# A hybrid decoder layer on eight cores: weight loads from a rearranged layout, early projections in one-bank pieces, and a last output tile in parts

## The chip, the cores and the metric

The kernel runs on all 8 cores of one Trainium2 chip. Every core has the same program and its own data: one prompt sequence of 2048 tokens and 16 sample tokens. The metric is the device time of the slowest core in microseconds (us).

A program on all cores has a second, slower state in some executions: the cores of one die get a lower clock, and the run is longer by a tenth or more. A median is over all runs of its kernel, so it can hold a slow one; the text says where. Tile numbers count from 0, so "tile 15" is the sixteenth and last full tile. TensorE is the matrix engine, VectorE, ScalarE and GpSimd the other compute engines, and SyncE (SP) here only issues transfers and waits for them. SBUF is the on-chip memory that holds the operands; PSUM is the memory that TensorE writes its results to, in banks that hold 512 fp32 columns here. In the profile their names are PE (PEld for weight loads), DVE, ACT, POOL and SP; a "q" after a name means the engine's sequencer (the part that issues transfers, waits and runs control instructions).

## The reference, cut to what matters

```python
def hybrid_layer(x, mem_k, mem_v, ...):              # x: (tokens, 1024) fp32
    u = rmsnorm(x, norm_g)
    proj = u @ w_in                                  # 8704 columns = 68 blocks of 128
    lx, lg, sb, scg, sh, sg, q, qg, mg = jnp.split(proj, SPLIT_POINTS, axis=-1)
    # A: causal conv(4) over lx, gated linear recurrence, times silu(lg), @ lru_wo
    # B: sb * causal conv(3) over (scg*sh), times silu(sg), @ sconv_wo
    # C: 4-head attention of q into 256 memory tokens, times silu(qg), @ xa_wo
    # [cut] the three branches are merged by sigmoid gates made from mg,
    # then one output projection @ w_out, the residual, and a final rmsnorm
```

Outputs are the normalised tokens (`y_prompt`, `y_sample`), the memory keys and values, and the new recurrence and convolution states. All are fp32; the matmuls run in bf16.

## The kernel before

The kernel records all its operations as tasks with a planned duration and a priority. Its own list scheduler then fixes one order per engine when the program is built. Where the next instruction of such a list has to wait, what stands behind it is held up with it; the run without pieces below shows what that costs TensorE (15.4 us of waits for scaled input tiles in the first 70 us, against 9.7 with pieces).

The input tiles. Each of the 16 prompt tiles (128 tokens) and the sample tile is loaded, squared and summed on ScalarE, given its reciprocal root on GpSimd (`rstd`), scaled, and transposed by eight TensorE instructions into `uT`.

```python
        def rstd(col, nr, prio):
            st = stat[0:nr, col:col + 1]
            G.pool(lambda e: e.tensor_scalar(out=st, in0=st, scalar1=1.0 / D, scalar2=EPS, op0=ALU.mult, op1=ALU.add),
                   0.2, [t_st[col]], [t_st[col]], prio)
            t_rs.append(G.pool(lambda e: e.tensor_tensor(out=st, in0=st, in1=cst[0:nr, 2:3], op=ALU.pow), 0.5,
                               [t_st[col], m_cst.t], [t_st[col]], prio))

        def p0(ti, src, nr, dst, gcols, tdst, prio, wait):
            x_, xn_, ps = Handle(xring), Handle(xnring), Handle(PS)      # PS: ring of 4 buffers of two PSUM banks
            # [cut] load from SP's queue, Square with sum on ScalarE, rstd on GpSimd,
            # scale on VectorE or GpSimd, 8 transposes, evacuation with gain on VectorE
```

The weights. GpSimd issues the load of a block of 128 columns of `w_in`, with a cast from fp32 to bf16. For each of 128 partitions and 8 row groups, it has 128 values in a row: 1024 pieces of 256 bytes as written.

```python
        def wload(ap, prio):
            k = ap.shape[1]
            hw = Handle(w2ring if 2 <= state["nw"] < 6 else wring)
            G.dma("pool", [(lambda: hw.ap[:, 0:k * 128].rearrange("p (k c) -> p k c", k=k), ap)], k * 65536 * 1.18, [], [hw.tok], prio, None)
            # [cut]

        def w_in_cols(c0):
            return w_in.rearrange("(k p) c -> p k c", p=128)[:, :, c0:c0 + 128]

        def unit(lhs, nk, rhs, u, reads, prio, hold=(), split=False):
            ps = Handle(PS)
            # [cut] 688 token columns as two halves of 344 (one PSUM bank each), 8 matmuls per half;
            # three such units cover the 2064 tokens
```

The last stage takes the 16 prompt tiles in order and the sample tile last.

```python
        for ti in range(17):
            # [cut] 16 matmuls of 512 columns, residual on VectorE, Square with sum on ScalarE
            rstd(col, nr, P)
            last = G.dve(lambda e, y_=y_, nr=nr, col=col: e.scalar_tensor_tensor(
                out=y_.ap[0:nr, :], in0=y_.ap[0:nr, :], scalar=stat[0:nr, col:col + 1], in1=fgb[0:nr, :], op0=ALU.mult, op1=ALU.mult), 1024,
                [y_.tok, t_st[col], m_fgb.t], [y_.tok], P)
            G.dma("sp", [(dst, lambda y_=y_, nr=nr: y_.ap[0:nr, :])], nr * 4096, [y_.tok], [], P, None)

        G.run(S, verbose)
        S.finish(block)     # then the program ends: every engine drains and meets the others at a barrier
```

The softmax here doesn't subtract the row's maximum and nothing guards it: scores larger than these inputs give would overflow.

Of the kernel before, what the change touches and what calls it, by code (L numbers as in the profile page):

```python
# [32 lines left out]
KVP = 10  # L33

# [121 lines left out]
class Ring:  # L156
    def __init__(self, name, aps, toks, sem=None):
        self.name = name
        self.aps = aps
        self.toks = toks  # L160
        self.sem = sem
        self.n = len(aps)
        self.avail = [0.0] * self.n
        self.busy = [False] * self.n


class Handle:
    __slots__ = ("ring", "phys", "left", "tok", "last")

    def __init__(self, ring):  # L170
        self.ring = ring
        self.phys = None
        self.left = 0
        self.last = 0.0
        self.tok = Tok(ring.name, handle=self)

    @property
    def ap(self):
        return self.ring.aps[self.phys]
# [13 lines left out]
class Graph:  # L193
# [85 lines left out]
    def dma(self, q, pairs, nbytes, reads, writes, prio, sem):  # L279
        return self._add(q, (0.95 if q == "pool" else 0.45) * len(pairs), None, reads, writes, prio, dma=(pairs, nbytes, sem))  # L280
# [29 lines left out]
    def run(self, S, verbose=False):  # L310
# [11 lines left out]
        while left:  # L322
            best = None
            for e, cands in ready.items():
# [5 lines left out]
                for t in cands:  # L330
# [3 lines left out]
                    for h in t.hs:  # L334
                        if h.phys is None:
                            a = 1e18
                            ring = h.ring
                            for i in range(ring.n):
                                if not ring.busy[i] and ring.avail[i] < a:
                                    a = ring.avail[i]  # L340
                            if a > r:
                                r = a
# [22 lines left out]
            for h in t.hs:  # L365
                if h.phys is None:
                    ring = h.ring
                    i = min((i for i in range(ring.n) if not ring.busy[i]), key=lambda i: ring.avail[i])
                    ring.busy[i] = True
                    h.phys = i  # L370
# [13 lines left out]
            if t.dma is not None:  # L384
                q, o = ("sw", "hw") if t.eng == "pool" else ("hw", "sw")
                a, n = max(dmafree[q], end + 0.8), t.dma[1] / 240e3
                both = min(2 * n, max(0.0, dmafree[o] - a))
                dmafree[q] = a + n + both / 2
                fin = dmafree[q] + 2.3
            for h in t.hs:  # L390
                h.left -= 1
                h.last = max(h.last, fin)
                if h.left == 0:
                    h.ring.busy[h.phys] = False
                    h.ring.avail[h.phys] = h.last
# [8 lines left out]
            mp = lambda k: k if k.handle is None else k.handle.ring.toks[k.handle.phys]  # L404
            reads, writes = [mp(k) for k in t.reads], [mp(k) for k in t.writes]
# [17 lines left out]
def build_program(verbose=False):  # L423
# [13 lines left out]
    st_h = din("st_h", [TS, W])  # L437
    st_lc = din("st_lc", [TS, 3 * W])
    st_sc = din("st_sc", [TS, 2 * W])
    norm_g = din("norm_g", [D])  # L440
    mem_norm_g = din("mem_norm_g", [D])
    w_in = din("w_in", [D, IN_COLS])
    lru_conv_w = din("lru_conv_w", [4, W])
    lru_conv_b = din("lru_conv_b", [W])
    lru_wa = din("lru_wa", [NCH, 128, 128])
    lru_ba = din("lru_ba", [W])
    lru_wx = din("lru_wx", [NCH, 128, 128])
    lru_bx = din("lru_bx", [W])
    lru_lambda = din("lru_lambda", [W])
    lru_wo = din("lru_wo", [W, D])  # L450
    sconv_w = din("sconv_w", [3, W])
    sconv_wo = din("sconv_wo", [W, D])
    xa_wk = din("xa_wk", [D, XW])
    xa_wv = din("xa_wv", [D, XW])
    xa_wo = din("xa_wo", [XW, D])
# [7 lines left out]
    o_ph = dout("o_ph", [1, W])  # L463
    o_plc = dout("o_plc", [3, W])
    o_psc = dout("o_psc", [2, W])
    o_sh = dout("o_sh", [TS, W])
    o_slc = dout("o_slc", [TS, 3 * W])
    o_ssc = dout("o_ssc", [TS, 2 * W])

    es = ExitStack()  # L470
    with es:
# [108 lines left out]
        def ring(name, mems, dma=False):  # L580
            if dma:
# [5 lines left out]
        PS = Ring("psum", [p[:] for p in psum], [Tok(f"psum{i}") for i in range(4)])  # L587
# [17 lines left out]
        m_prg = Mem("prg", PERM + 1792, 128, F32)  # L605
        m_prt = Mem("prt", PERM + 2304, 128, F32)
        prg, prt = m_prg.ap[0:16, :], m_prt.ap[0:66, :]
        t_pg = m_pT.tok("pTg")
        dsem("prg")
        dsem("prt")  # L610
        G.dma("sp", [(prg[0:8, :], norm_g.rearrange("(r c) -> r c", c=128)), (prg[8:16, :], mem_norm_g.rearrange("(r c) -> r c", c=128))],
              8192, [], [m_prg.t], -190, "prg")
        h = Handle(PS)
        G.pe([lambda e, h=h: e.transpose(h.ap[:, 0:16], prg, ident[0:16, 0:16])], 0.1, [m_prg.t, m_ident.t], [h.tok], -150)
        G.dve(lambda e, h=h: e.tensor_copy(pT[:, 0:16], h.ap[:, 0:16]), 16, [h.tok], [t_pg], -150)

        def params():
            plist = [(lru_conv_w, 0, 24, "k (n c) -> (k n) c"), (lru_conv_b, 24, 6, None), (lru_ba, 30, 6, None),
                     (lru_bx, 36, 6, None), (lru_lambda, 42, 6, None), (sconv_w, 48, 18, "k (n c) -> (k n) c")]
            G.dma("sp", [(prt[r0:r0 + nr, :], v.rearrange(pat, c=128) if pat else v.rearrange("(r c) -> r c", c=128))  # L620
                         for v, r0, nr, pat in plist], 42000, [], [m_prt.t], 20, "prt")
            G.after(G.tasks[-1], t_xd[10])
            h = Handle(PS)
            G.pe([lambda e: e.transpose(h.ap[:, 0:66], prt, ident[0:66, 0:66])], 0.3, [m_prt.t, m_ident.t], [h.tok], 30)
            G.dve(lambda e: e.tensor_copy(pT[:, 16:82], h.ap[:, 0:66]), 66, [h.tok], [m_pT.t], 30)


        def wload(ap, prio):
            k = ap.shape[1]
            hw = Handle(w2ring if 2 <= state["nw"] < 6 else wring)  # L630
            G.dma("pool", [(lambda: hw.ap[:, 0:k * 128].rearrange("p (k c) -> p k c", k=k), ap)], k * 65536 * 1.18, [], [hw.tok], prio, None)
# [5 lines left out]
        def w_in_cols(c0):  # L637
            return w_in.rearrange("(k p) c -> p k c", p=128)[:, :, c0:c0 + 128]

        def unit(lhs, nk, rhs, u, reads, prio, hold=(), split=False):  # L640
# [6 lines left out]
            if split:  # L647
                for b in range(2):
                    c = u * UW + b * BLK
                    t = G.pe([mm(k, b) for k in range(nk)], nk * 0.1465, [r for r in reads if r not in t_uT] + utoks(c, c + BLK), [ps.tok],  # L650
                             prio + 0.1 * b)
                    t.xgate = [t_tr[i] for i in range(17) if i * 128 < (u + 1) * UW] if b == 0 else []
            else:
                G.pe([mm(k, b) for k in range(nk) for b in range(2)], nk * 2 * 0.1465, reads, [ps.tok], prio, hold)
# [10 lines left out]

        def proj(c0, prio, lead=30.0, hold=((), (), ())):
            hw, lhs = pre.pop(c0) if c0 in pre else wload(w_in_cols(c0), prio - lead)
            return [unit(lhs, KC, uT, u, [hw.tok] + usl(u), prio + 2.4 * u, hold[u], prio < 60) for u in range(NU)]
# [27 lines left out]
        def p0(ti, src, nr, dst, gcols, tdst, prio, wait):  # L696
            x_, xn_, ps = Handle(xring), Handle(xnring), Handle(PS)
# [12 lines left out]
            def tr(kc):  # L710
# [6 lines left out]
                [ps.tok, t_pg], [tdst], prio)  # L717
# [5 lines left out]
        for i in range(17):  # L723
            if i >= 6:
                wait = [w_toks[min(i - 5, len(w_toks) - 1)]]
            elif i >= 3:
                wait = [x_toks[i - 3]]
            else:
                wait = []
            nr = 128 if i < 16 else TS  # L730
            src = xp[i * 128:(i + 1) * 128, :] if i < 16 else xs[:, :]
            x_toks.append(p0(i, src, nr, uT[:, :, i * 128:i * 128 + nr], pT[:, 0:8], t_uT[i], -100 + i, wait))
            while len(w_toks) < len(first) and len(w_toks) <= i:
                hw, lhs = wload(w_in_cols(first[len(w_toks)]), -100 + i)
                pre[first[len(w_toks)]] = hw, lhs
                if len(w_toks) >= 1:
                    G.after(G.tasks[-1], t_rs[i])
                w_toks.append(hw.tok)
                last = G.tasks[-1]
# [4 lines left out]
        params()  # L744


        m_sin = Mem("sin", m_xc.off, 4608, F32)
        sin = m_sin.ap
        for k in ("sin", "out"):
            dsem(k)  # L750
        t = G.dma("sp", [(sin[0:TS, 0:2304], st_lc[:, :]), (sin[0:TS, 2304:3072], st_h[:, :]),
                      (sin[0:TS, 3072:4608], st_sc[:, :])], 300000, [], [m_sin.t], 25, "sin")
        G.after(t, t_xd[15])
        o_slc3 = o_slc.rearrange("b (k c) -> b k c", k=3)
        st_lc3 = st_lc.rearrange("b (k c) -> b k c", k=3)
        o_ssc3 = o_ssc.rearrange("b (k c) -> b k c", k=2)
        st_sc3 = st_sc.rearrange("b (k c) -> b k c", k=2)
        t_dram = [Tok(f"dram{i}") for i in range(8)]
        t = G.dma("sp", [(o_slc3[:, 0:2, :], st_lc3[:, 1:3, :]), (o_ssc3[:, 0:1, :], st_sc3[:, 1:2, :])], 150000,
                  [], [t_dram[0]], 30, "out")  # L760
        G.after(t, t_rs[18])
        blocks_ = []
        for n in range(NCH):
            blocks_ += [k * W + n * 128 for k in range(3)] + [2304 + n * 128] + [3072 + k * W + n * 128 for k in range(2)]
        h = Handle(PS)
        t_sit = []
        for g0 in (0, 18):
            def trs(gi, g0=g0, h=h):
                c0 = blocks_[g0 + gi]
# [531 lines left out]
```

## Time and profile before

| | before |
|---|---|
| time, median of 3 runs | 767.55 us (767.3 to 767.73) |
| span of the profiled core (core 7, the slowest) | 764.4 us |
| TensorE busy | 719.3 us (94%) |
| sum of TensorE's work at its undisturbed pace | 700.4 us |
| time lost on TensorE by 60 / 110 / 400 us | 29.7 / 34.0 / 54 us |
| last matmul ends | 755.8 us |
| from there to the end | 8.6 us |

The fourth and fifth rows are worked out from the trace. A matmul in an undisturbed series starts a fixed time after the one before it (56 ns at 128 columns, 146 at 344, 216 at 512). The sum over all matmuls is the work. "Lost" is the time that has passed less the work done by then; half-clock time counts as lost too. This is a better ledger than "busy", because a matmul at half clock is busy twice as long.

These lines are from the page of the kernel before. They are the span, each engine's busy time with its instruction count, the shares of the chain of waits, the group of `w_in` loads as GpSimd issues them (busy us, mean ns of one | idle time before), and the same loads with size and us from issue to landing.

```profile
span 764.4 us, 12999 instructions; the slowest of 8 cores (758.2 to 764.4 us)
...
PE 719.3 (94%) x4771; PEld 456.5 (60%) x4771; DVE 403.8 (53%) x386; ACT 345.0 (45%) x408; POOL 246.4 (32%) x303
...
PE 85%; DMA 6%; ACT 4%; issue 2%; DVE 2%; POOL 1%; SPq 0%; POOLq 0%; ACTq 0%; DVEq 0%
...
L134 POOL DMA_DIRECT2D R<-w_in x68 | 61.5, 904 | 262.5 <-PE PP L645 250.7
...
R<-w_in POOLq DMA_DIRECT2D x68, 256.0 KB, 5.1
```

TensorE carries the kernel. The 6% of DMA in the chain lie in the head, and one issue of a weight load costs GpSimd 904 ns.

The queue table of the first 70 us of before: packets, MB, and the time that the packets took as a share of the 16 DMA engines.

```profile
q0 software_dynamic: 13819, 3.49, 56.2%
q1 hardware_dynamic: 2767, 9.55, 41.3%
```

The two shares add up to 97.5%, so transfers bind the head. The software queue (the weights, issued by GpSimd) moves 3.5 MB in 13,819 packets and takes more of the engines than the 9.6 MB of the hardware queue. The mean packet of 256 bytes took 46 ns there; over the whole run, the mean packet of 2048 bytes on the same queue took 201 ns, so eight times the bytes in 4.4 times the time. The Trainium skill, "DMA: Bandwidth & Descriptors", Specifications, says that transfers below 512 bytes miss the line rate; this trace agrees.

Three stretches of before, from the view of busy time by stretch: the stretch in us, its length, then busy us (and instructions) of PE, PEld, DVE, ACT and POOL, the granted TensorE clock, the DMA share and GB/s.

```profile
20.00:30.00 10.00, 7.08 (x36) 4.41 (x37) 4.13 (x4) 0.00 (x0) 4.22 (x6) 1.00 0.96 158
30.00:60.00 30.00, 26.53 (x205) 17.78 (x204) 13.71 (x12) 15.62 (x26) 17.32 (x27) 0.95 1.10 190
...
110.00:400.00 290.00, 276.89 (x1805) 175.64 (x1806) 184.79 (x151) 213.47 (x215) 46.28 (x63) 0.99 0.32 31
```

From 20 to 30 us TensorE did 36 matmuls and from 30 to 60 us 205, while the DMA engines were full.

Two lines of before's timeline of TensorE: start us, us taken, engine, line, operation, out<-in, count, and in brackets the idle time before it and what ended it.

```profile
24.74 5.52 PE L645 MATMUL PP<-R 128*128 128x344 bf16 x20
...
67.04 0.61 PE L711 MATMUL PP<-R 128*128 128x128 bf16 x8 [0.79 <-POOL R L703]
```

The first projection starts only at 24.74 us, and its 20 matmuls take 276 ns each, almost twice their undisturbed 146: the array is at half clock. The Trainium skill, "TensorE: Matmul & The Clock Gate", Part 1, says that the array runs at half rate until it has had some 3.4 us of sustained work. The trace agrees in kind: on the eight cores the first matmul at full pace came between 26.2 and 29.8 us, 2.0 to 5.0 us after the core's first projection had begun. The second line is the transposes of the last full input tile.

```profile
L141 SPq EVENT_SEMAPHORE  x54: 17/17/17, 761.5 to 764.1; - x54
...
L471 POOLq DRAIN  x1: 3108/3108/3108, 759.0 to 759.0; - x1
...
L471 SPq DRAIN  x1: 7/7/7, 764.2 to 764.2; - x1
```

A drain is the instruction that stands last in each engine's list, ahead of the closing barrier; in these traces none ends before its engine's last operation. SP's drain comes at 764.2 us, 8.4 us after the last matmul. The last store had landed 1.15 us before that, at 763.0: what lasted was SP's list of 54 waits, which SP took 2.69 us to step through (0.05 us each) once it had issued that store, though none of them held it up. All eight cores show the same. GpSimd's drain takes 3.1 us, or 2.55 us after its last operation (759.04 + 0.53). It is over at 762.1, two microseconds before SP gets to its own: it costs nothing here.

### The profile page before, as it was taken

The page shows a single profiled execution, that of the slowest core. Times are in us where ns is not written, and L with a number is a line of the kernel's source. Part 1 is how long each engine was busy: PE and PEld are TensorE (multiplying, and loading weights), DVE is VectorE, ACT ScalarE, POOL GpSimd, SP SyncE. Part 2 cuts the span into 40 slices and gives each one's busy share as a digit, 9 for nine tenths or more (in the row PEclk, how much of TensorE's full clock was granted, in tenths as well). Part 3 has the DMA queues.
Part 4 walks back from the last instruction along what each step waited for, and adds up shares of the span by engine and source line. Part 5 has one row for each costly group of instructions (what it writes and reads, how often), then busy time and mean ns, then how long its engine had stood idle before and what let it go on. Part 6 is the DMA issues. An engine that isn't in the chain of part 4 may idle for free.

```text
span 764.4 us, 12999 instructions; the slowest of 8 cores (758.2 to 764.4 us)
## 1 busy us (share of the span) xinstructions
PE 719.3 (94%) x4771; PEld 456.5 (60%) x4771; DVE 403.8 (53%) x386; ACT 345.0 (45%) x408; POOL 246.4 (32%) x303
## 2 busy tenths in 40 slices
PE   2889999989999989989999999999999999999995
PEld 1556656556566646646666666666666666665442
DVE  3354343846749638736976789842223122223765
ACT  4247379686696587687663211121111211112332
POOL 5555201201202102102114256553555464423221
PEclk9999999999999999999999999999999999999998
DMA  9999944412512332403324588865294849036933
GB/s 198 173 193 164 134 87 43 43 15 28 52 19 28 32 34 28 41 8 39 39 22 83 55 170 175 181 94 56 26 147 53 123 48 86 6 121 213 301 142 141
DMA packets 108601, 69.48 MB, mean 91 GB/s; under 512 B 94003, under 2 KB 96197, under 8 KB 108523
## 3 DMA queue, kind: packets, MB, share of 16 engines
q0 software_dynamic: 97760, 31.60, 39.7%
q1 hardware_dynamic: 10779, 37.06, 14.3%
q8 instruction: 39, 0.64, 0.3%
q14 instruction: 23, 0.19, 0.1%
HBM read 90.53 MB, written 9.82 MB: 131 GB/s over the span
## 4 chain that ended last, share of the span: by engine, by line
PE 85%; DMA 6%; ACT 4%; issue 2%; DVE 2%; POOL 1%; SPq 0%; POOLq 0%; ACTq 0%; DVEq 0%
PE PP L645 73%; PE PP L1227 8%; DMA R<-xp 3%; DMA R<-w_in 3%; PE PP L994 2%; ACT R L848 1%; PE PP L986 1%; DVE R L835 1%; ACT R L989 1%; ACT R L699 0%; POOL R L693 0%; POOL R L703 0%; PE PP L771 0%; PE PP L1122 0%; ACT R L832 0%
## 5 line engine op out<-in xcount | busy, mean ns | idle before, releaser
L645 PE MATMUL PP<-R 128*128 128x344 bf16 x4104 | 615.3, 311 | 6.8 <-ACT R L848 4.0
L645 PEld LDWEIGHTS PP<-R 128*128 128x128 bf16 x4104 | 401.7, 98 | 215.4 <-issue 16.2
L1179 ACT ACTIVATE R<-PP 128x688 f32<-128x688 f32 x72 | 53.6, 744 | 210.0 <-PE PP L645 205.2
L134 POOL DMA_DIRECT2D R<-w_in x68 | 61.5, 904 | 262.5 <-PE PP L645 250.7
L1188 DVE SCALAR_TENSOR_TENSOR R<-R,PP 128x688 f32<-128x688 f32 x72 | 62.3, 869 | 137.9 <-PE PP L645 130.0
L1227 PE MATMUL PP<-R 128*128 128x512 bf16 (+1 forms) x272 | 59.0, 379 | 0.0
L1192 POOL TENSOR_TENSOR R<-R 128x688 f32<-128x688 f32 x24 | 41.2, 1721 | 39.8 <-DVE R L1188 38.0
L1197 POOL TENSOR_TENSOR R<-R 128x688 bf16<-128x688 f32 x24 | 40.0, 1689 | 18.6 <-DVE R L1188 17.2
L1227 PEld LDWEIGHTS PP<-R 128*128 128x128 bf16 (+1 forms) x272 | 26.4, 97 | 32.2 <-issue 0.4
L835 DVE SCALAR_TENSOR_TENSOR R<-R 128x2048 f32<-128x2048 f32 x18 | 42.3, 2349 | 5.4 <-ACT R L832 4.2
L1236 ACT ACTIVATE R<-R 128x1024 f32<-128x1024 f32 (+1 forms) x17 | 18.0, 1057 | 46.3 <-DVE R L1231 46.3
L714 DVE TENSOR_TENSOR R<-PP,R 128x1024 bf16<-128x1024 bf16 (+1 forms) x19 | 22.2, 1174 | 21.4 <-PE PP L711 18.8
L711 PE MATMUL PP<-R 128*128 128x128 bf16 (+1 forms) x152 | 14.1, 248 | 19.2 <-DVE R L703 14.2
L1231 DVE SCALAR_TENSOR_TENSOR R<-PP,R 128x1024 f32<-128x1024 f32 (+1 forms) x17 | 20.8, 1224 | 20.6 <-PE PP L1227 20.6
L691 POOL TENSOR_SCALAR R<-R 128x1 f32<-128x1 f32 (+1 forms) x36 | 8.0, 222 | 72.8 <-ACT R L1236 44.5
L890 DVE TENSOR_TENSOR R<-PP,R 128x688 f32<-128x688 f32 x18 | 15.6, 873 | 28.1 <-PE PP L645 28.1
L848 ACT ACTIVATE R<-PP,R 128x688 f32<-128x688 f32 x36 | 27.4, 835 | 5.0 <-PE PP L645 5.0
L896 DVE SCALAR_TENSOR_TENSOR R<-R 128x2048 f32<-128x2048 f32 x12 | 28.2, 2346 | 0.9 <-ACT R L893 0.7
L862 DVE TENSOR_TENSOR_SCAN R<-R 128x2048 f32<-128x2048 f32 x6 | 26.5, 4421 | 0.4
L699 ACT ACTIVATE R<-R 128x1024 bf16<-128x1024 f32 (+1 forms) x19 | 20.1, 1056 | 14.6 <-DMA R<-xp 14.4
L1002 DVE TENSOR_TENSOR R<-PP,R 128x512 f32<-128x512 f32 x16 | 11.0, 687 | 27.0 <-ACT R L1000 27.0
L711 PEld LDWEIGHTS PP<-R 128*128 128x128 bf16 (+1 forms) x152 | 11.0, 111 | 23.3 <-issue 23.0
(133 smaller groups left out, 579.5 us busy)
## 6 DMA issues: line engine op xcount, KB each, us to landing
R<-w_in POOLq DMA_DIRECT2D x68, 256.0 KB, 5.1
R<-xp SPq DMA_DIRECT2D x32, 512.0 KB, 6.6
R<-ck SPq DMA_DIRECT2D x16, 512.0 KB, 4.7
y_p<-R SPq DMA_DIRECT2D x16, 512.0 KB, 3.0
R<-cv POOLq DMA_DIRECT2D x16, 256.0 KB, 7.5
R<-w_out POOLq DMA_DIRECT2D x8, 256.0 KB, 7.8
R<-xa_wo POOLq DMA_DIRECT2D x14, 128.0 KB, 4.1
R<-lru_wo POOLq DMA_DIRECT2D x8, 192.0 KB, 4.8
```

The costliest lines, as they stand in the source:

```text
L134: eng.dma_start(out=out, in_=in_).then_inc(sems[semkey], 16)
L645: return lambda e: e.matmul(ps.ap[:, b * 512:b * 512 + BLK], lhs(k), rhs[:, k, c:c + BLK], start=(k == 0), stop=(k == nk - 1))
L711: return lambda e: e.transpose(ps.ap.bitcast(BF16)[:, kc * 128:kc * 128 + nr], xn_.ap[0:nr, kc * 128:(kc + 1) * 128], identb[0:nr, 0:nr])
L835: G.dve(lambda e, k=k: e.scalar_tensor_tensor(out=xc[:, 0:T], in0=lxp[:, k:k + T], scalar=cw(k), in1=xc[:, 0:T], op0=ALU.mult, op1=ALU.add ...
L848: G.act(lambda e, ps=ps, dst=dst, u=u, bcol=bcol: e.activation(out=cols(dst, u), in_=pv(ps), func=AF.Tanh, scale=0.5, bias=dv[:, bcol:bcol ...
L862: G.dve(lambda e: e.tensor_tensor_scan(out=xc[:, 0:T], data0=thr[:, 0:T], data1=thi[:, 0:T], initial=0.0, op0=ALU.mult, op1=ALU.add), T, t ...
L896: G.dve(lambda e, k=k: e.scalar_tensor_tensor(out=cy[:, 0:T], in0=cinp[:, k:k + T], scalar=sw(k), in1=cy[:, 0:T], op0=ALU.mult, op1=ALU.ad ...
L1179: G.act(lambda e, ps=pg[u], th_=th_: e.activation(out=b3(th_.ap), in_=pv(ps), func=AF.Tanh, scale=0.5), UW, [pg[u].tok], [th_.tok], Px - E ...
L1188: G.dve(lambda e, zp=zp, th_=th_, dst=dst: e.scalar_tensor_tensor(out=b3(dst.ap), in0=b3(th_.ap), scalar=1.0, in1=pv(zp), op0=ALU.add, op1 ...
L1192: G.pool(lambda e, acc=acc, th_=th_: e.tensor_tensor(out=acc.ap, in0=acc.ap, in1=th_.ap, op=ALU.add), 1.6, [acc.tok, th_.tok], [acc.tok], Px)
L1197: G.pool(lambda e, acc=acc, th_=th_, u=u, j=j: e.tensor_tensor(out=mT[:, j, u * UW:(u + 1) * UW], in0=acc.ap, in1=th_.ap, op=ALU.add), 1.6 ...
L1227: return lambda e: e.matmul(ps.ap[0:nr, b * 512:(b + 1) * 512], mT[:, k, c0:c0 + nr], wo[:, k, b * 512:(b + 1) * 512], start=(k == 0), sto ...
```

## The change

The intent has four parts.

1. The host rearranges the weights, so that a `w_in` block is 128 rows of 2048 bytes as written.
2. Seven early projections are computed in pieces of 256 tokens (two input tiles) with one PSUM bank each, so that TensorE can start when two tiles are there. PSUM can be taken by one bank or by two. The loads are paced for two queues of equal speed.
3. States and parameters come and go in the layout the kernel needs, so that their transposes on TensorE fall away.
4. The sample tile moves before the last four prompt tiles and is computed in four column groups of the array. The last prompt tile is finished in parts of 512, 256 and 256 columns, its two halves are stored from two queues, and its root is taken on GpSimd from three partial sums.

The core of the diff, with cuts marked:

```diff
@@ weight loads and layout
         def wload(ap, prio):
-            k = ap.shape[1]
+            k = ap.shape[1] // 128
             hw = Handle(w2ring if 2 <= state["nw"] < 6 else wring)
-            G.dma("pool", [(lambda: hw.ap[:, 0:k * 128].rearrange("p (k c) -> p k c", k=k), ap)], k * 65536 * 1.18, [], [hw.tok], prio, None)
+            G.dma("pool", [(lambda: hw.ap[:, 0:k * 128], ap)], k * 65536, [], [hw.tok], prio, None)
@@
         def w_in_cols(c0):
-            return w_in.rearrange("(k p) c -> p k c", p=128)[:, :, c0:c0 + 128]
+            return w_in[c0 // 128]
@@ on the host
+    def rows(a, width):
+        a = f(a)
+        k, n = a.shape[0] // 128, a.shape[1] // width
+        return f(a.reshape(k, 128, n, width).transpose(2, 1, 0, 3).reshape(n, 128, k * width))
@@ [cut: lru_wo, sconv_wo, xa_wo, xa_wk, xa_wv, the gate weights likewise; par, st_T, o_T in place of on-chip transposes]
@@ pieces
+        def pieces(c0, prio, split):
+            if not split:
+                return [Piece(ps, u) for u, ps in enumerate(proj(c0, prio))]
+            hw, lhs = pre.pop(c0) if c0 in pre else wload(w_in_cols(c0), prio - 30)
+            out = []
+            for i in range(8):
+                ps, c = Handle(PS, 1), i * 256
+                n = 256 if i < 7 else TT - c
+                [cut: 8 matmuls of n columns, allowed once the tiles they read are transposed]
@@ pacing and the scheduler's model of the queues
-            if i >= 6:
-                wait = [w_toks[min(i - 5, len(w_toks) - 1)]]
-            elif i >= 3:
-                wait = [x_toks[i - 3]]
-            [cut]
+            while len(w_toks) < len(first) and len(w_toks) < i + LEAD:      # LEAD = 2
+                hw, lhs = wload(w_in_cols(first[len(w_toks)]), -200 + i)
+                [cut]
-                a, n = max(dmafree[q], end + 0.8), t.dma[1] / 240e3
-                [cut]
+                rate = 155e3 if start < 58.0 else 280e3
+                dmafree[q] = max(dmafree[q], end + 0.8) + t.dma[1] / rate
@@ last stage
+        def halves(ti, x_, dst, need, P):
+            [cut: three parts of 512, 256, 256 columns, each with its own residual, Square and gain]
+            G.pool(lambda e: e.tensor_scalar(out=st(3), in0=st(0), scalar1=st(1), scalar2=EPS, op0=ALU.add, op1=ALU.add), 0.2,
+                   [t_l[0], t_l[1]], [t_l[3]], P - 20)
+            G.pool(lambda e: e.tensor_tensor(out=st(4), in0=st(3), in1=st(2), op=ALU.add), 0.2, [t_l[2], t_l[3]], [t_l[4]], P - 20)
+            G.pool(lambda e: e.tensor_tensor(out=st(4), in0=st(4), in1=cst[:, 2:3], op=ALU.pow), 0.5, [t_l[4], m_cst.t], [t_l[4]], P - 20)
+            [cut: first half scaled on VectorE, second half on ScalarE]
+            for i, q in enumerate(("sp", "act")):
+                G.dma(q, [(dst[:, i * 512:(i + 1) * 512], lambda i=i: out[i].ap[:, 0:512])], 262144, [out[i].tok], [], P, None)
-        for ti in range(17):
+        for pos, ti in enumerate(list(range(12)) + [16, 12, 13, 14, 15]):
+            [cut]
+            if ti == 15:
+                halves(ti, x_, dst, need, P)
+                continue
```

## The prediction

> **What bounds the kernel now.** TensorE: busy 719.3 of 764.4 us (chain of waits: 85%). Start-to-start times of undisturbed matmuls in the trace (56 ns at 128 columns, 146 at 344, 216 at 512) add up to about 700 us. The last matmul ends at 755.8 us, so some 55 us are lost before it, and 8.6 us follow it. By the timeline: 24 us by 30 us, 30 by 60, 34 by 110, 54 by 400 (ScalarE and softmax waits), 55 at the end.
>
> The head is bound by DMA: from 10 to 60 us the windows show the 16 engines fully busy. In the first 70 us' queue table the software queue takes 56% of them, 46 ns for a 256-byte packet, 2.9 us of all engines for a w_in block. An x tile (128 packets of 4096 bytes, 199 ns) takes 1.6 us. The Trainium skill, "DMA: Bandwidth & Descriptors", Specifications, says transfers under 512 bytes miss line rate; the trace agrees (256 bytes in 46 ns, 2048 in 200). TensorE runs at half clock until 28 us (287 ns for 344 columns), as "TensorE: Matmul & The Clock Gate", Part 1, describes for an array without sustained work.
>
> **What the change does.**
> 1. Weights come rearranged by the host: a w_in block becomes 128 packets of 2048 bytes, an estimated 1.6 us, not 2.9. Thirteen blocks free 17 us of DMA in the head.
> 2. Seven early projections run in 256-column pieces (estimate 109 ns a matmul, interpolated), one bank each, once two tiles are there. Per x tile TensorE has about 24 matmuls and 8 transposes, 3.1 us, against an x and a w load, 3.3 us. The instruction order has pieces after the second tile's transposes; before, after the sixth. Estimate: first piece at 15 us, full clock by 21, then 0.2 to 0.4 us lost per tile. Lost by 60 us: about 20 in place of 29.7. Gain 10 us (6 to 13), all on the critical path.
> 3. TensorE work removed: 36 state transposes (2.3 us), output and parameter transposes (0.8). The sample tile's 3.46 us becomes 32 matmuls in four column groups, about 0.9 us (existing such groups start 3 to 4 ns apart). Extra piece matmuls add 0.3. Sum 5.4 us, all critical.
> 4. Tail: the last tile's chain is shorter, but VectorE must still finish the tile before (1.27 us), then issue and landing, about 3.3 us. Estimate 7.8 us, not 8.6: gain 0.8.
> 5. Added: 5 us of ScalarE evacuations in the head, where it has room. Recurrence and attention are reordered, not lightened: the 20 us lost there stay, give or take 3.
>
> **Prediction.** 767.5 - 10 - 5.4 - 0.8 = about 751; I say 750.5 us, range 745 to 756.5. Faster by over 2%: 0.58; within 2%: 0.41; slower: 0.01.
>
> **What would show it.** (1) 128 packets a w_in load, not 1024. (2) First 256-column matmul near 15 us, pitch 109 ns, full clock by 21; the sixteenth x tile's transposes (67 us before) at about 60. (3) No state transposes; sample tile about 0.9 us. (4) About 7.8 us from last matmul to end. (5) ScalarE waits between 120 and 400 us about unchanged.
>
> **What would make it wrong.** If big packets from both queues on all cores slow each other, tiles come later and the static order makes TensorE wait. ScalarE's order may stall tiles. Attention's new order may win or lose some us.

## More of the kernel before

The end of before, first from the timeline (the sample tile's residual, its root on GpSimd, its final scale and its store), then the closing instructions by line (engine, operation, count: duration in ns min/median/max, first and last start in us). L141 is the list of waits that `S.finish` gives SP, one for each semaphore by which transfers report their end.

```profile
756.04 1.21 DVE L1231 SCALAR_TENSOR_TENSOR R<-PP,R 16x1024 f32<-16x1024 f32 x1 [1.13 <-PE PP L1227]
...
759.04 0.53 POOL L693 TENSOR_TENSOR R<-R 16x1 f32<-16x1 f32 x1
759.75 1.27 DVE L1240 SCALAR_TENSOR_TENSOR R<-R 16x1024 f32<-16x1024 f32 x1 [1.30 <-POOL R L693]
761.09 0.33 SPq L134 DMA_DIRECT2D y_s<-R  x1
```

## The result, and the profile after

| | before | after |
|---|---|---|
| time, median | 767.42 us (4 runs) | 758.7 us (4 runs, a slow one among them; 758.48 without it) |
| fast runs | 767.25 to 767.73 | 757.05, 758.48, 758.92 |
| span of the slowest core | 764.4 us | 755.5 us |
| TensorE work | 700.4 us | 695.1 us |
| lost by 60 / 110 / 400 us | 29.7 / 34.0 / 54 us | 20.2 / 23.3 / 45.5 us |
| last matmul ends | 755.8 us | 742.1 us |
| from there to the end | 8.6 us | 13.4 us |

The fourth run of after was slow: 840.63 us, with clocks of 0.869 to 0.905 on one die. It is left out of the ratio. A ratio here, and everywhere below, is the mean time of one kernel's fast runs over that of the other's fast runs of the same rounds, so not quite the ratio of the medians quoted. It is 0.9879, with a 95% interval of 0.9859 to 0.9898. That is within 2%. A repeat in 5 rounds gave 758.64 against 769.0 us, ratio 0.9865 (0.9852 to 0.9878). The prediction of 750.5 us was wrong, and so was its range, which ended at 756.5; the outcome that it gave 0.58 to, faster by over 2%, did not come.

The page of after, the same parts:

```profile
span 755.5 us, 13274 instructions; the slowest of 8 cores (751.5 to 755.5 us)
...
PE 709.3 (94%) x4863; PEld 462.5 (61%) x4863; DVE 398.9 (53%) x390; ACT 346.4 (46%) x445; POOL 222.3 (29%) x303
...
PE 88%; ACT 3%; DMA 3%; issue 2%; POOL 1%; DVE 1%; POOLq 0%; SPq 0%; ACTq 0%; DVEq 0%
...
L135 POOL DMA_DIRECT2D R<-w_in x68 | 37.8, 556 | 258.3 <-PE PP L644 245.1
...
R<-w_in POOLq DMA_DIRECT2D x68, 256.0 KB, 4.4
```

DMA's share of the chain fell from 6% to 3%, and an issue now costs GpSimd 556 ns in place of 904. Nothing on this page says that the end has become longer: POOLq stands at 0% in the chain of both.

The queue table of the first 70 us of after:

```profile
q1 hardware_dynamic: 2976, 9.99, 44.8%
q0 software_dynamic: 2173, 4.17, 39.8%
```

The software queue moved more bytes than before, in 2,173 packets in place of 13,819, and took less of the engines' time.

The three stretches of after:

```profile
20.00:30.00 10.00, 7.21 (x76) 6.23 (x74) 3.35 (x4) 6.02 (x13) 4.04 (x7) 1.00 1.03 256
30.00:60.00 30.00, 29.66 (x309) 26.36 (x307) 15.55 (x15) 20.31 (x50) 15.31 (x30) 1.00 0.92 232
...
110.00:400.00 290.00, 276.31 (x1791) 175.13 (x1789) 195.17 (x160) 212.07 (x212) 44.72 (x66) 0.98 0.21 33
```

In the two early stretches TensorE does 76 and 309 matmuls in place of 36 and 205 (many are shorter now, 256 columns in place of 344). In the middle it does slightly fewer than before.

TensorE's timeline in the head of after:

```profile
16.19 1.86 PE L688 MATMUL PP<-R 128*128 128x256 bf16 x8 [1.48 <-DVE R L738]
...
27.14 2.78 PE L688 MATMUL PP<-R 128*128 128x256 bf16 x24
...
61.44 0.61 PE L735 MATMUL PP<-R 128*128 128x128 bf16 x8 [0.18 <-POOL R L727]
```

The first piece starts at 16.19 us at half clock (230 ns a matmul), full pace is reached at 18.9 us on this core (by 23.6 on the last), and the last full tile's transposes come at 61.44 us in place of 67.04. Over the cores the first piece starts between 16.2 and 17.7 us. The head does what it was meant to do.

Now the end of after: the timeline, then the closing instructions by line (engine, operation, count: duration in ns min/median/max, first and last start in us), then SP's last long wait (who waited, for whom: total us, times, longest us).

```profile
738.50 3.64 PE L1206 MATMUL PP<-R 128*128 128x512 bf16 x24
...
744.51 1.28 DVE L1264 SCALAR_TENSOR_TENSOR R<-R 128x1024 f32<-128x1024 f32 x1
744.79 1.42 POOL L1221 TENSOR_TENSOR R<-R 128x1 f32<-128x1 f32 x1
...
747.15 0.38 ACTq L135 DMA_DIRECT2D y_p<-R  x1
```

```profile
L142 SPq EVENT_SEMAPHORE  x57: 17/17/17, 747.3 to 750.5; - x57
...
L488 POOLq EVENT_SEMAPHORE  x2: 17/17/17, 755.3 to 755.4; - x2
L488 PEldq DRAIN  x1: 2368/2368/2368, 739.8 to 739.8; - x1
L488 POOLq DRAIN  x1: 10516/10516/10516, 744.8 to 744.8; - x1
...
L488 SPq DRAIN  x1: 7/7/7, 750.6 to 750.6; - x1
```

```profile
SPq L488 <- PEq L488: 4.9, 1, 4.9
```

The last store has landed at 750.1 us, and SP has stepped through its 57 waits and reached its drain at 750.6. But the span ends at 755.5. In between, every engine sits in the closing barrier and waits for GpSimd's drain, which takes 10.5 us, or 9.07 us after GpSimd's last operation (744.79 + 1.42) ended. The barrier's signals follow it at once, at 755.3 and 755.4. The last load that GpSimd issued had landed at 638.4 us, so no load of its own was still under way. The same 9.07 us appear on all eight cores; before it was 2.55.

The last fence is a lesson in reading waits. The view puts SP's last 4.9 us down to PE. TensorE's own drain, however, was over at 742.2; the engine that arrived last was GpSimd, and the wait view doesn't say so.

The ledger of the slowest core closes. Its last matmul ends 13.7 us earlier: 10.7 us less lost by 110 us, 5.3 us less work, 2.3 us more lost after 110 us. Its end part is 4.8 us longer. Together that is 8.9 us, the difference of the spans. These are the slowest cores of two runs; recounted over the cores with complete records, the mean loss by 110 us fell by 8.7 us (32.5 to 23.8), not 10.7.

### The profile page after: what moved, and what is told of

Read it like the earlier page. It is cut to its first block, busy times and chain, and to the rows that moved or that the text cites. A ratio compares the mean times of both kernels' runs of the same rounds, so it can differ in the third digit from the quotient of the medians.

```text
span 755.5 us, 13274 instructions; the slowest of 8 cores (751.5 to 755.5 us)
## 1 busy us (share of the span) xinstructions
PE 709.3 (94%) x4863; PEld 462.5 (61%) x4863; DVE 398.9 (53%) x390; ACT 346.4 (46%) x445; POOL 222.3 (29%) x303
## 4 chain that ended last, share of the span: by engine, by line
PE 88%; ACT 3%; DMA 3%; issue 2%; POOL 1%; DVE 1%; POOLq 0%; SPq 0%; ACTq 0%; DVEq 0%
PE PP L644 72%; PE PP L688 6%; PE PP L1250 5%; PE PP L988 2%; DMA R<-xp 1%; DMA R<-w_in 1%; ACT R L842 1%; PE PP L918 1%; PE PP L980 1%; PE PP L735 1%; ACT R L983 1%; POOL R L717 0%; DVE R L1255 0%; ACT R L992 0%; ACT R L1260 0%
## 5 line engine op out<-in xcount | busy, mean ns | idle before, releaser
L644 PE MATMUL PP<-R 128*128 128x344 bf16 x3768 | 561.5, 310 | 9.0 <-ACT R L842 4.6
L644 PEld LDWEIGHTS PP<-R 128*128 128x128 bf16 x3768 | 368.6, 98 | 201.0 <-issue 18.4
L135 POOL DMA_DIRECT2D R<-w_in x68 | 37.8, 556 | 258.3 <-PE PP L644 245.1
L688 PE MATMUL PP<-R 128*128 128x256 bf16 (+1 forms) x448 | 54.7, 276 | 4.7 <-DMA R<-w_in 1.9
L1250 PE MATMUL PP<-R 128*128 128x512 bf16 (+1 forms) x272 | 53.0, 367 | 0.0
L688 PEld LDWEIGHTS PP<-R 128*128 128x128 bf16 x448 | 42.9, 99 | 12.7 <-issue 6.1
L1250 PEld LDWEIGHTS PP<-R 128*128 128x128 bf16 (+1 forms) x272 | 24.1, 97 | 28.7 <-issue 0.6
L842 ACT ACTIVATE R<-PP,R 128x688 f32<-128x688 f32 x36 | 27.5, 834 | 5.7 <-PE PP L644 5.7
L735 PE MATMUL PP<-R 128*128 128x128 bf16 (+1 forms) x152 | 12.5, 230 | 12.9 <-DVE R L727 9.7
L1062 DVE TENSOR_TENSOR R<-R 128x1024 f32<-128x1024 f32 x16 | 22.1, 1383 | 3.3 <-DMA R<-ck 2.4
```

Source lines behind the costliest of these rows:

```text
L135: eng.dma_start(out=out, in_=in_).then_inc(sems[semkey], 16)
L644: return lambda e: e.matmul(ps.ap[:, b * 512:b * 512 + BLK], lhs(k), rhs[:, k, c:c + BLK], start=(k == 0), stop=(k == nk - 1))
L688: return lambda e: e.matmul(ps.ap[:, 0:n], lhs(k), uT[:, k, c:c + n], start=(k == 0), stop=(k == KC - 1))
L842: G.act(lambda e, ps=ps, dst=dst, u=u, bcol=bcol: e.activation(out=cols(dst, u), in_=pv(ps), func=AF.Tanh, scale=0.5, bias=dv[:, bcol:bcol ...
L1250: return lambda e: e.matmul(o_, mT[:, k, c0:c0 + nr], wo[:, k, b * w:(b + 1) * w], start=(k == 0), stop=(k == KC - 1))
```

## The experiments

What made GpSimd's drain long? I had four theories, which the expectations call by these letters.

- **A**: the split last tile. It gives GpSimd two extra sums, one of them reading its addend through a pointer, and the last operations are slow.
- **B**: the last tile on GpSimd has 128 partitions now, where before the 16 rows of the sample tile came last.
- **C**: the store from ScalarE's queue, a second queue to be settled.
- **D**: the weight loads that GpSimd issued. They are lighter now, and something of them is still to be settled at the end.

A fifth, **E**, stands in some expectations as the rival of D: a fixed cost of any drain of this program.

The head raised a second question: do the pieces or the new layout give the gain? In all, twelve runs were made, of ten changed kernels and two repeats, in four groups; each group shares its runs of the kernel before, whose medians were 767.57, 768.57, 767.27 and 769.0 us. All results were correct.

### The last tile like the others

```diff
-            if ti == 15:
-                halves(ti, x_, dst, need, P)
-                continue
```

> The kernel after, with its last tile (tile 15) computed like the others: one wide group, one square, the usual two GpSimd operations, one store. Theory A (the GpSimd operations that the split tile adds, a sum with a pointer and a sum of two, make GpSimd's closing drain long): the drain falls from 10.5 us to about 3, the end comes 8.6 to 9 us after the last matmul (13.4 after the change, 8.6 before it), and the time falls from 758.7 to about 754. Theory B (the drain is long because the last GpSimd operation covers 128 partitions, where before it covered the 16 of the sample tile): the drain stays near 10.5 us, the end comes about 13.7 us after the last matmul, time 758.5 to 759.5. Theory C (the store issued from ScalarE's queue makes it long): as A.

Measured in 3 rounds: 757.63 us, ratio 0.9876 (0.986 to 0.9893). The closing drain, by line:

```profile
L488 POOLq DRAIN  x1: 9654/9654/9654, 746.0 to 746.0; - x1
```

It is still 9.07 us after the last operation, without split tile, extra sums or store from ScalarE's queue. So A and C fall. The end part was 13.1 us. SP reached its drain 8.97 us after the last matmul on every core, against 8.4 to 9.1 in after (the last stores had landed after 8.0 to 8.2, against 7.8 to 8.8). The split tile by itself thus gains nothing or a few tenths.

### The two sums of the split tile on VectorE

```diff
-            G.pool(lambda e: e.tensor_scalar(out=st(3), in0=st(0), scalar1=st(1), scalar2=EPS, op0=ALU.add, op1=ALU.add), 0.2,
-                   [t_l[0], t_l[1]], [t_l[3]], P - 20)
-            G.pool(lambda e: e.tensor_tensor(out=st(4), in0=st(3), in1=st(2), op=ALU.add), 0.2, [t_l[2], t_l[3]], [t_l[4]], P - 20)
+            G.dve(lambda e: e.tensor_scalar(out=st(3), in0=st(0), scalar1=st(1), scalar2=EPS, op0=ALU.add, op1=ALU.add), 1,
+                  [t_l[0], t_l[1]], [t_l[3]], P - 20)
+            G.dve(lambda e: e.tensor_tensor(out=st(4), in0=st(3), in1=st(2), op=ALU.add), 1, [t_l[2], t_l[3]], [t_l[4]], P - 20)
```

> The kernel after, with the two sums of the split last tile moved from GpSimd to VectorE; the power stays on GpSimd, the store stays on ScalarE's queue. Theory A (the two added GpSimd operations): drain about 3 us, time about 754. Theory B (128 partitions in the last GpSimd operation): drain 9 to 10.5 us, time 758 to 759. Theory C (the store from ScalarE's queue): drain stays about 10.5 us, time 758 to 759.

Measured in 3 rounds: 756.85 us, ratio 0.9865 (0.9851 to 0.988). The drain took 9.08 us after the last operation, so A falls again. The end part was 12.3 us; the stores had landed 8.1 to 8.5 us after the last matmul.

One thing did change: the power on GpSimd took 0.63 us in place of 1.42. In after a VectorE operation with two inputs in SBUF had begun 0.28 us before it and ran until 745.79 (timeline above); the power ended 0.42 us after that. Here the one that had begun before it was short and ended at 745.54, 0.22 us after the power's start, and the power ended 0.41 us after that; a longer one began only after the power. The Trainium skill, "SBUF — State Buffer", Who interferes with whom, says that such a VectorE operation contends with a GpSimd instruction that reads SBUF. The 1.42 us, the 0.63 us here, and the usual 0.55 elsewhere in the stage agree with that.

### The kernel before, with 128 partitions in the last tile's root

```diff
-        last = None
+        last = G.dve(lambda e: e.memset(stat[:, 36:37], 1.0), 1, [], [t_st[36]], -200) and None
-            rstd(col, nr, P)
+            rstd(col, 128, P)
```

> The kernel before, with one change: the two GpSimd operations of the last (sample) tile's statistics cover 128 partitions in place of 16 (the other rows are never used). Theory A and C: nothing moves, drain 3.1 us, time 767.4 within 0.5. Theory B: the drain grows from 3.1 to about 10.5 us, and as it starts 5.4 us before the end, the time rises by about 5 us to 772.5.

Measured in 3 rounds: 768.24 us, ratio 1.001 (0.998 to 1.004).

```profile
L471 POOLq DRAIN  x1: 3124/3124/3124, 763.2 to 763.2; - x1
```

The drain stays at 2.54 us after the last operation. B falls. Of the four, D remains, and the next kernels had to make it show itself.

### An early drain on GpSimd

```diff
+        G.pool(lambda e: e.drain(), 9.0, [t_mT[7][u] for u in range(NU)], [Tok("drained")], PF - 30)
```

This is one line ahead of the last stage, when all weight loads have been issued and GpSimd has room.

> The kernel after, with one drain instruction added on GpSimd after the last addition of the merge stage (about 690 us), where GpSimd has room. The runs so far show the closing drain lasting 9.07 us after the last GpSimd operation in every kernel with the rearranged weights and 2.55 us in both kernels with the old ones, whatever that last operation is. Theory D (the drain settles work left over from the weight loads issued by GpSimd, so settled early it isn't paid at the end): the added drain takes 8 to 9 us, the closing one under 2 us after its last operation, the end comes about 8.6 us after the last matmul in place of 13.4, the time falls by 4 to 5 us to about 753.5. Theory E (a fixed cost of any drain of this program): both take 9 us, the time stays or rises.

Measured in 3 rounds: 754.18 us (753.38 to 754.78), ratio 0.9802 (0.9782 to 0.9822). The added drain by its line, and the closing ones by theirs:

```profile
L1229 POOLq DRAIN  x1: 9049/9049/9049, 690.4 to 690.4; - x1
```

```profile
L488 POOLq DRAIN  x1: 1512/1512/1512, 746.6 to 746.6; - x1
...
L488 SPq DRAIN  x1: 7/7/7, 752.4 to 752.4; - x1
```

The 9.05 us have moved to 690.4 us, where nobody on the critical path waits for them. The closing drain ends 0.07 us after GpSimd's last operation, which it overlapped, and the span ends with SP again: 8.64 us from the last matmul, against 13.37. On five of the eight cores the last store had landed before SP was through its waits, and the end part is 8.64 us; on the other three SP still waited for that store, and it is 8.71 to 8.97. D is shown as far as this goes: what the drain settles was there by 690 us, and the last tile doesn't make it.

### The split tile's sums on VectorE, together with the early drain

The edit is that of the two kernels above together.

> The kernel after with the two sums of the last tile on VectorE (that run: 756.85 us, end 12.3 us after the last matmul, stores done after 8.6) and the drain added early as well. Theory D: end about 8.6 us after the last matmul, time about 753. Theory E: about 757 or more.

Measured in 3 rounds: 754.74 us (one run at 752.8, one slow at 891.33; 754.66 without the slow one), ratio 0.9801 (0.9775 to 0.9828). The end part was 8.4 to 9.2 us. There is no clear gain over the early drain alone: SP began its list of waits 0.5 us sooner, but on every core it then waited in it for the last store.

### Twenty-four more loads from GpSimd in the last stage

```diff
+        m_xt = Mem("xt", m_w[0].off, 16, BF16)
+        dsem("xt")
@@ in the loop over output tiles
+            if pos < 12:
+                G.dma("pool", [(m_xt.ap[:, 0:8], w_out[0:128, 0:8]), (m_xt.ap[:, 8:16], w_out[0:128, 8:16])], 8192, [], [m_xt.t], P, "xt")
```

The loads are useless on purpose; nobody reads what they bring.

> The kernel after, with 24 useless loads of 128 packets of 16 bytes issued by GpSimd in the last stage. Theory D in its simplest form (a cost for each load since the last settling, about 9.07 us over 126 loads, 0.07 us each): the closing drain grows by about 1.7 us to 10.8 us after the last GpSimd operation, and the time by as much. Theory E: 9.07 us unchanged. If it falls clearly below 9 us, only what the last loads were matters.

Measured in 3 rounds: 758.21 us, ratio 0.9851 (0.9826 to 0.9876).

```profile
L488 POOLq DRAIN  x1: 6439/6439/6439, 753.5 to 753.5; - x1
```

The drain fell to 4.99 us after the last operation, where a cost per load since the start would have raised it to 10.8. That simple form of D is refuted. (The time didn't fall with it: with the added loads GpSimd's last operation ended 4.9 to 11.2 us after the last matmul, in place of 4.1, and the stores landed 8.8 to 15.1 us after it.)

### A drain after each block of the merge stage

```diff
+            G.pool(lambda e: e.drain(), 1.0, [t_mT[j][2]], [Tok(f"drained{j}")], P)
```

> The kernel after, with a drain on GpSimd after each of the eight blocks of the merge stage. Theory D (each unsettled load adds to the next drain): each drain's length follows the number of loads issued since the one before, by my estimate about 0.07 us a load (9.07 us over 125 loads), so 0.4 to 1.2 us for the 6 to 16 loads of a block, more for the first, which settles what is left of the front stages; the closing drain then ends within 0.1 us of the last operation. Rival (a drain costs 9 us whatever came before, except directly after another): every one takes several us. The time is of no interest here.

Measured once: 755.62 us. On core 3, the drains, in order, and the loads that GpSimd had issued since the drain before:

| drain | 1 | 2 | 3 | 4 | 5 | 6 | 7 | 8 | closing |
|---|---|---|---|---|---|---|---|---|---|
| loads since the last | 64 | 6 | 11 | 10 | 15 | 11 | 8 | 0 | 0 |
| us | 5.29 | 0.54 | 0.94 | 4.81 | 4.96 | 0.94 | 0.69 | 0.05 | 0.08 after the last operation |

Five of the seven that had loads before them follow one rule, 0.083 to 0.09 us for each load since the last drain: 5.29 / 64 is 0.083, and 0.94 / 11 is 0.085. The fourth and fifth do not. They vary between 2.55 and 5.07 us over the cores, and the trace shows what they waited for: 1 to 4 of their loads were still under way when they began, and on all eight cores the fourth ended 0.45 us and the fifth 0.65 us after the last of these had landed. So a drain here also waits for loads under way.

### Twelve more loads

The edit is that of the 24 loads, with one load per tile in place of two.

> The kernel after with 12 useless loads (24 of them shortened the closing drain from 9.07 to 4.99 us). If each extra load takes away a like share: about 7.0 us. If loads add up until a store is full and a part of it is settled then: either about 9.9 us (not yet full) or about 4.1 (just settled).

Measured once: 753.65 us.

```profile
L488 POOLq DRAIN  x1: 5457/5457/5457, 745.9 to 745.9; - x1
```

This is 4.01 us after the last operation. With 125 loads (after) the drain cost 9.07 us, with 137 it cost 4.01, with 149 it cost 4.99. The step from 137 to 149 is 0.98 us, or 0.082 us a load: the rule of the drains above. Twelve more loads should have brought 9.07 to about 10.05; the fall to 4.01 means that about 6 us' worth was settled on the way. So the cost behaves like a sawtooth: it grows by the load, and at some point a part of it is settled while the kernel runs. By the rule, after ended with an estimated 107 unsettled loads (9.07 / 0.085), and before with an estimated 30 (2.55 / 0.085), if one of its loads of 1024 packets counts as a light one, which no run shows.

What is settled, and when, no run shows; in after and in the two kernels with added loads no issue of a load took over 1.03 us, so it does not show as a long issue. The Trainium skill, "DMA: Bandwidth & Descriptors", SWDGE vs HWDGE vs iDMA, says that GpSimd computes the descriptors of its own loads in software and appends them to rings in SBUF. A finite store that has to be cleared would fit both the sawtooth and the next experiment's drain, but it is only a reading.

### The old layout of `w_in` alone

```diff
-    w_in = din("w_in", [IN_COLS // 128, 128, D])
+    w_in = din("w_in", [D, IN_COLS])
-            return w_in[c0 // 128]
+            return w_in.rearrange("(k p) c -> p k c", p=128)[:, :, c0:c0 + 128]
@@ [cut: the matching view of the destination, and the host's array]
```

Everything else is as in after, and TensorE's order is the same.

> The kernel after, with the blocks of w_in loaded from the old layout (1024 packets of 256 bytes each), the same instruction order on TensorE. Drain: theory D in the form that large loads fill the descriptor store and so get settled on the way: about 2.5 to 4 us after the last operation, against 9.07. Head: TensorE had lost 20 us by 60 us with pieces and new layout, 29 with the new layout alone. If pieces alone carry the head's gain, 20 to 22 us; if they need the light loads, 27 or more (13 loads cost 17 us more of all DMA engines). My theory: they need them, 26 to 30 us. Time: 8 more in the head, 4.5 less at the end, about 761.

Measured in 3 rounds: 767.67 us, ratio 0.9978 (0.9958 to 0.9998). The closing drain, and TensorE's wait for the weights in the first 70 us (in after the same pair is 1.9 us):

```profile
L488 POOLq DRAIN  x1: 5133/5133/5133, 759.9 to 759.9; - x1
```

```profile
PE PP L688 <- DMA R<-w_in: 16.2, 3, 8.8
```

I had expected 26 to 30 us lost by 60 us and a time of about 761, and both were too low. Two things follow. First, with loads of 1024 packets the drain is 3.69 us after the last operation in place of 9.07, although the number of loads is the same: the layout changed what was left to the closing drain. But as the cost is a sawtooth, this doesn't show that light loads leave more as a rule: twelve more of them left 4.01. Second, the pieces without the light loads gain nothing. Up to 60 us, 32.6 to 35.3 us were lost on the cores whose matmul records are complete, more than in before (25.8 to 29.8 there). TensorE's order is the one planned for light loads; pieces with an order planned for heavy ones were not tried.

### The pieces alone taken out

```diff
         def pieces(c0, prio, split):
-            if not split:
+            if True:
```

> The kernel after, with the early projections back in units of 688 columns (weights still rearranged by the host). If the pieces carry the head's gain, TensorE has lost 27 to 30 us by 60 us as before (20.2 with pieces, 29.7 before) and the time rises to 766 or more. If the lighter weight loads carry it, about 21 us are lost by 60 us and the time stays within 1 us of 758.7. My theory: both are needed, about 24 us lost by 60 us, time about 762.5.

Measured in 3 rounds: 764.62 us, ratio 0.9967 (0.9952 to 0.9982). TensorE's longest wait in the first 70 us:

```profile
PE PP L735 <- DVE R L727: 15.4, 5, 10.1
```

TensorE waits for the input tiles as it did in before, and its first unit starts at 29.1 us. By 60 us, about 27.5 to 29.5 us were lost over the cores, as in before. I had expected about 24, and a time of 762.5, so I had credited the layout with some of the gain by itself. It gives almost none (about 1 us by 110 us, as a mean over cores): once the transfers are light, the order makes TensorE wait until units of 688 columns have their tiles. Each half of the change needs the other. The drain here was 9.07 us as well, so the pieces have no part in it.

### Repeats in five rounds

> The kernel after, unchanged, measured on the same chip and in the same rounds as the version with the early drain. All theories: about 758.5 us, ratio to before about 0.988, end 13.4 us after the last matmul.

> The kernel after with the early drain, again: theory D: about 754 us, 4 to 5 us under the kernel after of the same rounds, ratio to before about 0.982, clear of the 0.988 of the kernel after.

After, unchanged: 758.64 us, ratio 0.9865, end part 13.37 us. After with the early drain: 754.12 us, ratio 0.9808 (0.9795 to 0.9821), end part 8.64 us (one slow run, 846.66, left out). One of the eleven runs of before was slow too (902.42); it counts in the median of 769.0 and not in the ratios. No other version was clearly faster than the early drain: 754.66 us is the fast median with the sums on VectorE too, and 753.65 us the single run with twelve useless loads. It is 4.5 us faster than after and 1.8 to 2.1% faster than before; whether it passes 2% stays unclear.

## Why the prediction was wrong

The mechanism of the head was right, and so was most of the sum. The step that failed is item 4, the tail: it took the last tile's chain and the landing of its stores for what ends the kernel, at 7.8 us after the last matmul. What ended it was GpSimd's closing drain, at 13.1 us, and, with that out of the way, SP's closing waits, at 8.4 us.

**Item 1, light loads.** Right. A load of `w_in` is 128 packets, and the software queue's packets in the first 70 us fell from 13,819 to 2,173. What I missed is a consequence elsewhere: with these loads the closing drain is long (9.07 us with them, 3.69 with `w_in` from the old layout), at this number of loads.

**Item 2, pieces.** Right. Predicted: 20 us lost by 60 us, measured 20.2; gain 10, measured 9.5 by 60 us and 10.7 by 110 us on the slowest cores (7.3 and 8.7 as a mean over cores, within the stated 6 to 13). The first piece came at 16.2 us (predicted 15), full pace at 18.9 to 23.6 us over the cores (predicted by 21, which three of the eight missed by 0.4 to 2.6), the last tile's transposes at 61.4 us (predicted 60), and the pitch of a 256-column matmul was 109 ns as estimated.

**Item 3, work removed.** Right. Predicted 5.4 us, measured 5.3. The sample tile in four column groups took 0.98 us (predicted 0.9).

**Item 4, tail.** Wrong. Predicted 7.8 us from the last matmul to the end, where the chain of the last tile and its stores would decide it; measured 13.4. Two things stood in its place.

- The smaller one: even with the drain out of the way the end part is 8.64 us, no shorter than before (8.59 us), because SP's list of waits sets it. The chain of the last tile did get shorter: SP issued its last store 4.8 us after the last matmul in place of 5.3. But SP then steps through 57 waits in 3.24 us where before it had 54 in 2.69 us (0.37 us of it in a single step, at the same semaphore in every run, which no run explains). The 0.5 us gained are lost again there. The last stores themselves had landed 7.8 to 8.4 us after the last matmul in the run with the early drain, and decided only on three of its cores. No run with a shorter list was made. This is 0.8 us of the miss.
- The larger one: GpSimd's closing drain of 9.07 us after its last operation set the end on every core. The early drain moved it away and the end part fell from 13.37 to 8.64. This is 4.7 us of the miss.

**Item 5, middle.** Within its margin, but against me: 2.3 us more lost between 110 us and the end, of a stated 3. One wait is new. Near 129 us a projection waits 2.38 us for the softmax's exponential on ScalarE (who waited, for whom: total us, times, longest us), on all eight cores of after and of its repeat, and on none of before or of the kernel without pieces:

```profile
PE PP L644 <- ACT R L983: 2.4, 1, 2.4
```

On six of the eight cores the clock falls to half for 3.4 us about when it ends (0.3 us before to 1.1 us after). Stretches at half clock between 110 and 400 us averaged 7.7 us a core after and 3.8 before; half of that difference, 1.9 us, is lost time. Other waits became shorter (those for the gate's activation on ScalarE, 4.0 to 3.2 us). So the reordered attention costs TensorE a wait that the prediction left open ("may win or lose some us"); no experiment moved it, so how much of the 2.3 us it makes is not shown.

Added up, the miss is 758.7 less 750.5, or 8.2 us: 5.6 from the tail, 2.3 from the middle, 0.8 from rounding 751.3 down to 750.5, and 0.7 back from the head. The remaining tenths are within the spread of runs. Without the drain (754.12 us) the time lies inside the predicted range, still 3.6 us above its centre.

The closing instructions of before already showed the 3.1 us drain on GpSimd, free only because SP reached its own two microseconds later. I had costed the tail as a chain of tile operations and a store, and never asked which engine would reach the closing barrier last.

## What to carry to other kernels

Read the closing instructions of every engine as part of the critical path: the span ends with the last engine at the barrier, and that may be an engine with nothing left to compute. Loads that GpSimd issued can leave something to be settled by its drain at the end, and how much depends on their number and layout in no simple way (9.07 us here, 4.01 with twelve more loads); one early drain, put where GpSimd has room, was worth 4.5 us here. And when a change has two halves (lighter loads, and an order that uses them early), try each alone before crediting either: here neither half alone gave the head more than about 1 us.

## What the Trainium skill lacked or had wrong

- "VectorE: DVE Perf Modes", The DRAIN you can't avoid, tells VectorE's pipeline flush from the runtime's own drains, which it gives as a constant of about 12 ns on all five engines. The drain that closes a program's own list is neither, and is missing there: SP's took 7 ns, but GpSimd's took 3.1 us in before and 10.5 us in after, 2.55 and 9.07 us of it after its last operation. The latter set the end of the kernel.
- No page says what a drain on GpSimd costs after loads that GpSimd issued; it belongs to "DMA: Bandwidth & Descriptors", SWDGE vs HWDGE vs iDMA. The runs show 0.082 to 0.09 us a load since the last drain (64 loads: 5.29 us), partly settled at points along the way (125 loads: 9.07 us; 137: 4.01; 149: 4.99), and up to 5.07 us for 10 to 15 loads when some were still under way.
- "Perfetto Trace Analysis" has nothing on the closing barrier of a program. In after, the waits put SP's last 4.9 us down to PE, while GpSimd's drain ended at 755.3 us and the barrier opened 0.1 us later. The drains' own records have to be compared. Nor does it say what a list of satisfied waits costs: SP stepped through 54 in 2.69 us.
